# Attention logits: key low parts stored in both partition halves, and the softmax division moved behind the values' products

## The chip, the cores and the metric

The kernel runs on one core of one Trainium2 chip. The metric is device time in microseconds; the kernel before took 1897.31 us (median of 3 runs, 1897.23 to 1901.52).

## The reference, cut to what matters

The program is one layer of a hybrid decoder: a gated delta rule (mixer A), sparse attention over the 256 best keys of each query (mixer B), a merge, and an MLP. The change lies in mixer B's attention over a prompt of 1024 tokens, 8 query heads of 64 numbers, 2 key/value heads:

```python
kb = rope(rms_norm(bk.reshape(b, t, N_KV_B, HD_B), k_norm_g), pos)
...
logits = jnp.einsum('bqngd,bqknd->bqngk', qg, k_sel, preferred_element_type=jnp.float32) * (HD_B ** -0.5)
logits = jnp.where(valid[:, :, None, None, :], logits, -jnp.inf)
p = jax.nn.softmax(logits, axis=-1)
o = jnp.einsum('bqngk,bqknd->bqngd', p.astype(v.dtype), v_sel)
```

The kernel does not gather: it computes logits against all earlier keys and adds a mask that leaves out those not selected.

## The kernel before, in words

**Precision by parts.** TensorE multiplies float32r numbers here. To keep float32 accuracy each operand is kept as two parts, hi (rounded) and lo (the rest), and a product is made of several passes that add up in PSUM.

**The stages.** `mixers()` makes norms, projections, the indexer's scores and masks, and the delta rule. In it, `kv_chain` (line 495) makes keys and values by token tile of 128 rows and writes their parts to DRAM (`kvd`, 640 columns a tile). At its end `pool_chain` (line 412) loads `kvd` into the tile `kv` (lines 436 to 438). Then `rest()` (line 1601) runs the attention, the merge of the two mixers, and the MLP.

**The attention.** 16 groups (token tile t, kv head n), in the order of tiles 7, 6, 0, 1, 2, 5, 4, 3. A group of tile t has L = 128 (t + 1) keys and 4 query heads.

- `logit_chain` (line 1620): loads the queries `q3`, rotates them (`rope`, GpSimd and VectorE), transposes and splits them into `qS`. `split_heads` (line 361) puts hi on 64 partitions and lo on the other 64. For each head and each 512 keys there are two passes into the PSUM tile `pat`: line 1646 with 128 rows (query hi and lo, against key hi, which `kv` holds twice, once in each half of the partitions), and line 1648 with 64 rows (query hi against key lo; lo of kv head n lies in half n only). VectorE adds the mask and takes the maximum (line 1649). Then come, per head: the maximum of two chunks, a product of maximum and scale (line 1654), the exponential with its sum on ScalarE, a reciprocal, and a scaling of all L exponentials by it (line 1658), on ScalarE for odd heads and on VectorE for even ones.
- `value_chain` (line 1664): for each 128 keys, 4 transposes (`ptp`), a split into `ph` (ScalarE) and `pl` (VectorE), two passes into `po`. At the end ScalarE copies `po` to `oT`, and a DMA writes it to `obd`.
- `merge_chain` and the MLP read `obd` back and fill the other engines' time: `pdn<-oa` is the projection of mixer A, `pdn<-ob` that of mixer B, `pdn<-mix` the output projection.

**The order of the work.** Each engine runs its instructions in program order. That order is written by a planner, `Flow` (line 51): it holds several chains (`value_chain` first, then `logit_chain`, `pool_chain`, `merge_chain`, `norm_chain`, `mlp_chain`) and emits the first whose inputs should be there by then. It prices a step by the sizes of its outputs (lines 71 to 80) and takes 0.8 of their sum plus 0.6 us for each engine used as the step's delay (line 113). A pass over 64 rows costs the same in it as one over 128. `logit_chain` may be at most two groups ahead of `value_chain` (line 1624). All loads and stores but those of `kv` are issued by SyncE, in one queue.

Of the kernel before, what the change touches and what calls it, by code (L numbers as in the profile page):

```python
# [8 lines left out]
F32 = mybir.dt.float32  # L9
# [7 lines left out]
P = 128  # L17
# [3 lines left out]
NS = 8  # L21
NT = NP_ + NS
C0, CN, CM = (0, 384, 768), (384, 384, 264), 384                # chunks of tokens
# [6 lines left out]
FIRST, REST = [2, 0], [1]                                         # chunks of tokens in the order of the merge  # L30
# [7 lines left out]
def tok(t):  # L38
    """columns of token tile t (8: the samples)"""
    return slice(NP_, NT) if t == 8 else slice(t * P, (t + 1) * P)  # L40
# [10 lines left out]
class Flow:  # L51
    """Emits several chains of steps in one program order: a step of the first chain whose inputs should
    be there by then, by rough estimates of what each engine has been given so far."""
# [32 lines left out]
    def run(self, chains, cur):  # L86
        """chains: generators in order of priority; they yield None or an Event to wait for; each has its own pools"""
# [37 lines left out]
def program(ctx, tc, I, O, dbg=None, upto=99):  # L125
# [10 lines left out]
    xnp = ExitStack()                                             # the mixers' x and numbers  # L136
# [17 lines left out]
    def stage(name, side=None, **tags):  # L154
        """pools of one part of the program; tags: PSUM tiles by tag"""
# [8 lines left out]
    def copy(eng, out, in_, scale=None):  # L164
        """PSUM or SBUF to SBUF on ScalarE or VectorE"""
# [20 lines left out]
    def split(hi, lo, src, heng="act", leng="dve"):  # L186
        """src -> its float32r parts; lo = src - hi is exact"""
        copy(heng, hi, src)
        (V if leng == "dve" else G).tensor_tensor(lo, src, hi.bitcast(F32), OP.subtract)

    # ------------------------------------------------------------ constants
    jp = cs2.tile([P, P], I32, name="jp")                         # column - row
# [5 lines left out]
    tri = cs2.tile([P, P], F32, name="tri")                       # row <= column  # L198
# [4 lines left out]
    # ------------------------------------------------------------ weights  # L203
    def block(src, name, lo="pool", spare=False):
        """[P, kt, n] of weights -> their float32r parts, a list of [P, 2, n] by 128 rows"""
# [10 lines left out]
    def unit(src, name, lo="pool"):  # L216
        """weights in blocks of 512 numbers a partition"""
# [6 lines left out]
    def dense(ws, xin, evac, chunks=range(3)):  # L224
        """products of 128 columns of weights with all tokens, channels on partitions; a step per chunk"""
# [9 lines left out]
    # ------------------------------------------------------------ scratch in DRAM  # L235
    qd = dr.tile([8, P, 512], F32, name="qd")                     # attention queries by token tile
    qid = dr.tile([8, P, 512], F32, name="qid")                   # indexer queries by token tile
    sd = dr.tile([NS, 3, 512], F32, name="sd")                    # the samples' indexer and attention queries; k v ki
    cqd = dr.tile([12, P, NT], F32, name="cqd")                   # q, k, v of mixer A, channels on partitions
    azd = dr.tile([P, 4, NT], F32, name="azd")  # L240
    gd = dr.tile([16, P, NT], F32, name="gd")                     # the merge gates
    obd = dr.tile([2, P, 4, NP_], F32, name="obd")                # mixer B by kv head: rows of both parts of the values, head, token
# [3 lines left out]
    def oat(t):  # L246
        """mixer A's rows for a token tile"""
        c = t % 3 * P
        return oad[t // 3][:, :, c:c + (NS if t == 8 else P)]


    # ------------------------------------------------------------ kept over both mixers
    kvd = dr.tile([8, P, 640], F32, name="kvd")                   # parts of keys and values by token tile, as part 4 takes them
    off = {t: sum((u + 1) * P for u in range(2, t)) for t in range(2, 9)}
    right = {}                                                    # pools from the other end of the SBUF
    wab = cs2.tile([P, 9, 8], F32, name="wab")
    wsg = cs2.tile([P, 9, 8], F32, name="wsg")
    abt = cs2.tile([P, 9, 8], F32, name="abt")                    # logits of beta and the decay by token
    G.memset(abt[:, 8, :], 0.0)
    cs_s = cs2.tile([P, 12, NS], F32, name="cs_s")                # q, k, v of the samples in mixer A  # L260
    az_s = cs2.tile([P, 4, NS], F32, name="az_s")
    ssA = cs2.tile([P, 2, 9, 4], F32, name="ssA")                    # sums of squares of q and k heads
    G.memset(ssA[:, :, 8], 1.0)

    qsc = cst.tile([P, 9, 8], F32, name="qsc")                    # 1 / norm of the attention queries, over 8
# [10 lines left out]
    def seg(t):  # L276
        return cur["sc"][:, off[t]:off[t + 1]]                    # scores of token tiles 2..7, then their masks

    # ------------------------------------------------------------ mixer A: numbers by token and head
# [6 lines left out]
    # columns: 0 gc, 1 rk, 2 rk beta, 3 beta, 4 exp(gc); 5 -gc, 6 -rk beta exp(gc), 7 rk exp(gl - gc), 8 exp(gl)  # L286
# [3 lines left out]
    Ud = dr.tile([NCH, P * 4 * P + P], F32, name="Ud")            # padded: diagonal blocks at one stride over all chunks  # L290
    decd = dr.tile([NCH, P, 4, P], F32, name="decd")              # the decays of each chunk
# [29 lines left out]
    def xat(t):  # L321
        """x^T of token tile t: [P, parts, 128 rows, tokens]"""
# [17 lines left out]
    def gains(pool=None):  # L340
        """(q, k) gains x (plain, halves swapped)"""
# [1535 lines left out]
```

## Time and profile before

| what | value |
|---|---|
| median of 3 runs | 1897.31 us (1897.23 to 1901.52) |
| the profiled execution, its span (first to last instruction) | 1899.1 us |
| TensorE busy | 1826.1 us, 96% of the span |
| TensorE weight loads | 1719.9 us, 91% |
| VectorE / ScalarE / GpSimd busy | 58% / 45% / 32% |
| logits, first to last pass | 805.3 to 1051.8 us |

In the profile PE is TensorE's matmuls, PEld its weight loads, DVE VectorE, ACT ScalarE, POOL GpSimd, SP SyncE. Every instruction has line 82, that of the planner's recorder, so one goes by the names of tiles. Durations of PE rows are modelled and overlap: what a pass costs is read from the start of one row to the start of the next.

### The profile page before, as it was taken

To read this page: it belongs to the slowest core of one execution; us is meant where nothing else is said; L and a number is where in the kernel's file an instruction comes from. 1 tells how busy PE (TensorE), PEld (TensorE's weight loads), DVE (VectorE), ACT (ScalarE), POOL (GpSimd) and SP (SyncE) were. 2 spreads that over 40 slices of the span, in tenths; PEclk is the share of its full clock that TensorE was granted. 3 is DMA by queue.
4 is the path that set the end of the run, shared out by engine and by line. 5 is a ranking of instruction groups with operands and counts; after the bars stand their busy time and mean duration, and the time that the engine had idled before them with its cause. 6 is when DMAs were issued, how large, how long until landed. Compare 5 with 4: busy or idle time off the path is not lost. (4 is left out here: it accounts for less than half of the span.)

```text
span 1899.1 us, 32840 instructions
## 1 busy us (share of the span) xinstructions
PE 1826.1 (96%) x11894; PEld 1719.9 (91%) x11894; DVE 1109.7 (58%) x3116; ACT 852.1 (45%) x1945; POOL 609.8 (32%) x749
## 2 busy tenths in 40 slices
PE   6999989899999999999999979999999999999998
PEld 5899979898998889878777879999999999999998
DVE  7767768998897985277889677222232323232323
ACT  5356675567787522256767634222222131313131
POOL 2334336614332461301433465222222121313130
PEclk9999999999999999999899989999999999999999
DMA  5335463215354444633664453111111111111112
GB/s 179 109 100 170 150 214 111 82 55 170 107 153 119 136 135 136 204 114 113 182 173 131 119 172 95 55 46 45 45 51 50 45 45 51 41 54 46 45 34 90
DMA packets 167764, 198.24 MB, mean 104 GB/s; under 512 B 29521, under 2 KB 112769, under 8 KB 167594
## 3 DMA queue, kind: packets, MB, share of 16 engines
q1 hardware_dynamic: 163314, 183.04, 32.0%
q0 software_dynamic: 4288, 13.11, 2.4%
q8 instruction: 93, 1.52, 0.3%
q14 instruction: 69, 0.57, 0.1%
HBM read 148.99 MB, written 47.21 MB: 103 GB/s over the span
## 5 line engine op out<-in xcount | busy, mean ns | idle before, releaser
L82 PE MATMUL pdn<-u,wc 128*128 128x384 f32 (+1 forms) x2304 | 367.3, 320 | 0.0
L82 PEld LDWEIGHTS pdn<-u,wc 128*128 128x128 f32 x2304 | 362.7, 188 | 0.1
L82 PE MATMUL pdn<-hn,wc 128*128 128x384 f32 (+1 forms) x2304 | 362.1, 319 | 0.0
L82 PEld LDWEIGHTS pdn<-hn,wc 128*128 128x128 f32 x2304 | 360.5, 188 | 0.3
L82 PE MATMUL pdn<-xn,wu 128*128 128x384 f32 (+1 forms) x1440 | 256.7, 331 | 3.2 <-ACT z L82 3.2
L82 DVE TENSOR_TENSOR hT<-hT,pdn 128x384 f32<-128x384 f32 (+1 forms) x216 | 110.5, 512 | 251.1 <-PE pdn L82 248.0
L82 PEld LDWEIGHTS pdn<-xn,wu 128*128 128x128 f32 x1440 | 231.6, 194 | 11.1 <-issue 5.3
L82 DVE SCALAR_TENSOR_TENSOR r<-pdn,rs 128x384 f32<-128x384 f32 (+1 forms) x96 | 49.4, 516 | 273.6 <-PE pdn L82 273.5
L82 POOL TENSOR_TENSOR u<-r,u 128x384 fp32r<-128x384 f32 (+1 forms) x96 | 89.4, 932 | 274.3 <-ACT u L82 247.6
L82 PE MATMUL pa<-xn,wu 128*128 128x384 f32 (+1 forms) x864 | 158.0, 329 | 2.5 <-ACT a L82 2.5
L82 PEld LDWEIGHTS pa<-xn,wu 128*128 128x128 f32 x864 | 139.3, 193 | 4.5 <-ACT a L82 2.9
L82 ACT ACTIVATE r<-r 128x384 f32<-128x384 f32 (+1 forms) x96 | 47.1, 492 | 172.4 <-DVE r L82 171.7
L82 ACT ACTIVATE jka<-sc,nf 128x512 bf16<-128x512 f32 (+3 forms) x124 | 101.4, 821 | 33.5 <-DVE nf L82 19.7
L82 PE MATMUL pdn<-mix,wc 128*128 128x384 f32 (+1 forms) x576 | 96.3, 321 | 1.9 <-ACT mix L82 1.3
L82 PEld LDWEIGHTS pdn<-mix,wc 128*128 128x128 f32 x576 | 90.8, 188 | 3.6 <-ACT mix L82 1.7
L82 DVE SCALAR_TENSOR_TENSOR a<-u,cw,a 128x384 f32<-128x384 f32 (+1 forms) x108 | 76.2, 706 | 13.1 <-ACT a L82 12.4
L82 PE MATMUL pat<-kv,qS 128*128 128x512 f32 (+3 forms) x192 | 73.4, 431 | 3.2 <-DVE qS L82 3.1
L82 POOL TENSOR_TENSOR wu<-wu_4r,wu 128x512 fp32r<-128x512 f32 x32 | 42.8, 1336 | 104.3 <-ACT wu L82 96.2
L82 PE MATMUL pdn<-ob,wc 128*128 128x384 f32 (+1 forms) x288 | 57.6, 350 | 10.3 <-DVE ob L82 7.3
L82 DVE TENSOR_SCALAR_CACHE_REDUCE jk<-sc,cf 128x768 bf16<-128x768 f32 (+1 forms) x62 | 66.2, 1071 | 1.4 <-ACT jka L82 1.3
L82 PEld LDWEIGHTS pat<-kv,qS 128*128 128x128 f32 x192 | 36.4, 189 | 33.6 <-issue 25.0
L82 ACT ACTIVATE lg<-lg,st,qsc 128x1024 f32<-128x1024 f32 (+7 forms) x64 | 55.3, 864 | 22.2 <-DVE st L82 21.7
(904 smaller groups left out, 3350.8 us busy)
## 6 DMA issues: line engine op xcount, KB each, us to landing
wu_0r<-in_w_un SPq DMA_DIRECT2D x32, 256.0 KB
wu_4r<-in_w_un SPq DMA_DIRECT2D x32, 256.0 KB
gd<-g SPq DMA_DIRECT2D x32, 192.0 KB
ga<-gd SPq DMA_DIRECT2D x32, 192.0 KB
cqd<-a SPq DMA_DIRECT2D x24, 192.0 KB
xt<-in_x_prompt SPq DMA_DIRECT2D x8, 512.0 KB
obd<-oT SPq DMA_DIRECT2D x16, 256.0 KB
xt<-in_x_prompt SPq DMA_DIRECT2D x16, 256.0 KB
```

Of the source, the lines that this page charges most:

```text
L82: return f(*a, **k)
```

## The change

- Key lo parts of each kv head are stored in both halves of the partitions, like key hi. `kvd` and `kv` grow from 640 to 768 columns, with one transpose more per token tile, and the copy of the transposed keys grows from 384 to 512 columns.
- The second pass of the logits uses all 128 rows (query hi and lo against key lo), like the first.
- The queries are multiplied by their scale `qsc` on GpSimd before the rotation, so the exponential needs no scale.
- VectorE writes negated logits and takes the minimum; the second chunk starts from the first's minimum. This takes the place of two or three small VectorE instructions per head.
- The exponentials aren't divided by their sum. One reciprocal per group makes the 4 factors; `value_chain` transposes them (4 transposes of a column repeated over 128 columns), ScalarE copies them to `rb`, and VectorE multiplies `po` by `rb` where ScalarE copied before.
- Buffers: `lg` 10 to 9, `st` 3 to 4, `rb` in the place of `oT`.

The diff, without those hunks that only take out comments or rename sizes:

```diff
-                    kv = w([P, 640], "kvt", F32R)
+                    kv = w([P, 768], "kvt", F32R)
...
-                    V.tensor_tensor(kst[:, 2], ko3, kst[:, 0:2, 0].bitcast(F32), OP.subtract)
-                    split(kst[:, 3], kst[:, 4], bc(kio[:, i], 2))
+                    V.tensor_tensor(kst[:, 2:4], bc(ko3, 2, 2), kst[:, 0:2].bitcast(F32), OP.subtract)
+                    split(kst[:, 4], kst[:, 5], bc(kio[:, i], 2))
...
-                    for j in range(5):
-                        T.transpose((ptk if j < 3 else pti)[:, (j % 3) * P:(j % 3 + 1) * P],
+                    for j in range(6):
+                        T.transpose((ptk if j < 4 else pti)[:, (j % 4) * P:(j % 4 + 1) * P],
...
-                    copy("act", kv[:, :384], ptk[:, :384])
+                    copy("act", kv[:, :512], ptk)
...
+                G.tensor_tensor(q3, q3, bc(qsc[:, t, 4 * n:4 * n + 4], 64, 2), OP.mult)
                 qr = w([P, 4, 64], "qr")
                 rope(qr, q3, tab, P, 4)
-                qS = split_heads(qr, "qS", 2, n, "pa")
+                qS = split_heads(qr, "qS", 2, 0, "pa")
                 yield
-                st_ = small([P, 4, 4], "st", bufs=3)
+                st_ = small([P, 4, 4], "st", bufs=4)
...
-                        T.matmul(p3, qS[:, h], kv[:, bl, n * P:(n + 1) * P], start=True, stop=False)
-                        hi = slice(64 * n, 64 * n + 64)
-                        T.matmul(p3, qS[hi, h], kv[hi, bl, 256:384], start=False, stop=True)
-                        V.tensor_tensor_reduce(lg[:, c0:c0 + cn], pa[:, :cn], bias[:, c0:c0 + cn], 1.0, LOW,
-                                               op0=OP.add, op1=OP.max, accum_out=st_[:, c, h:h + 1])
-                    if nch == 2:
-                        V.tensor_tensor(st_[:, 0, h:h + 1], st_[:, 0, h:h + 1], st_[:, 1, h:h + 1], OP.max)
-                    scale = qsc[:, t, 4 * n + h:4 * n + h + 1]
-                    V.scalar_tensor_tensor(st_[:, 2, h:h + 1], st_[:, 0, h:h + 1], -1.0, scale, op0=OP.mult, op1=OP.mult)
-                    S.activation(lg[:, :L], lg[:, :L], AF.Exp, bias=st_[:, 2, h:h + 1], scale=scale,
-                                 accum_out=st_[:, 3, h:h + 1])
-                    V.reciprocal(st_[:, 1, h:h + 1], st_[:, 3, h:h + 1])
-                    copy("act" if h % 2 else "dve", lg[:, :L], lg[:, :L], st_[:, 1, h:h + 1])
+                        for a in range(2):
+                            T.matmul(p3, qS[:, h], kv[:, bl, (2 * a + n) * P:(2 * a + n + 1) * P], start=(a == 0), stop=(a == 1))
+                        V.tensor_tensor_reduce(lg[:, c0:c0 + cn], pa, bias[:, c0:c0 + cn], -1.0,
+                                               st_[:, c - 1, h:h + 1] if c else -LOW,
+                                               op0=OP.add, op1=OP.min, accum_out=st_[:, c, h:h + 1])
+                    S.activation(lg[:, :L], lg[:, :L], AF.Exp, bias=st_[:, nch - 1, h:h + 1], scale=-1.0,
+                                 accum_out=st_[:, 2, h:h + 1])
                     yield
+                V.reciprocal(st_[:, 3], st_[:, 2])
+                lgs.append(st_[:, 3])
...
+                pr = pst("prr", "pt")
+                for h in range(4):
+                    T.transpose(pr[:, h * P:(h + 1) * P], lgs[4][:, h:h + 1].to_broadcast([P, P]), ident)
+                rb = w([P, 512], "rb", bufs=2)
+                copy("act", rb, pr)
                 po = pst("po", "po")
...
-                oT = w([P, 512], "oT", bufs=2)
-                copy("act", oT, po)
-                dma(obd[n, :, :, tok(t)], h4(oT))
+                V.tensor_tensor(rb, po, rb, OP.mult)
+                dma(obd[n, :, :, tok(t)], h4(rb))
```

## Rows read from the trace of the kernel before

**Rows 1.** The page, part 1: busy time, share and instructions of each engine.

```profile
PE 1826.1 (96%) x11894; PEld 1719.9 (91%) x11894; DVE 1109.7 (58%) x3116; ACT 852.1 (45%) x1945; POOL 609.8 (32%) x749
```

**Rows 2.** Windows of the attention: length, busy of PE, PEld, DVE, ACT, POOL, clock, DMA.

```profile
840.00:880.00 40.00, 40.00 (x212) 30.71 (x210) 31.91 (x97) 28.70 (x49) 3.46 (x4) 1.00 0.33 102
...
930.00:980.00 50.00, 49.37 (x294) 38.28 (x293) 46.43 (x134) 36.76 (x78) 18.82 (x18) 1.00 0.63 176
...
sum 270.00, PE 262.63 PEld 209.93 DVE 217.67 ACT 182.20 POOL 72.68; mean PE 43.77 PEld 34.99 DVE 36.28 ACT 30.37 POOL 12.11
```

**Rows 3.** Tile pat: matmuls, ns min/median/max, first and last start, forms (rows*columns).

```profile
L82 PE MATMUL pat<-kv,qS x192: 221/440/687, 805.5 to 1051.8; 128*128 128x512 f32 x48, 64*128 64x512 f32 x48, 128*128 128x384 f32 x16, 64*128 64x384 f32 x16
```

**Rows 4.** Timeline, tile 7's first head: start, length, engine, operation, count, idle before.

```profile
805.49 2.53 PE L82 MATMUL pat<-kv,qS 128*128 128x512 f32 x6
...
805.80 0.18 PEld L82 LDWEIGHTS pat<-kv,qS 64*128 64x128 f32 x1 [0.30 <-issue]
...
807.94 2.04 PEld L82 LDWEIGHTS pdn<-oa,wc 128*128 128x128 f32 x12 [0.24 <-DVE st L82]
807.94 2.35 PE L82 MATMUL pdn<-oa,wc 128*128 128x384 f32 x12
```

**Rows 5.** Timeline of PE alone: chunks of 128 keys, transposes, chunks of 384 keys.

```profile
892.82 1.58 PE L82 MATMUL pat<-kv,qS 128*128 128x128 f32 x6
894.34 1.73 PE L82 MATMUL pdn<-oa,wc 128*128 128x264 f32 x12
...
940.94 1.27 PE L82 MATMUL ptp<-ident,lg 128*128 128x128 f32 x10
941.97 2.27 PE L82 MATMUL pat<-kv,qS 128*128 128x384 f32 x6
944.16 1.72 PE L82 MATMUL pdn<-ob,wc 128*128 128x264 f32 x12
```

**Rows 6.** Timeline of PE alone, the indexer's scores (psc), next to other products.

```profile
404.00 1.09 PE L82 MATMUL psc<-kiS,qiS 128*128 128x512 f32 x4
404.93 2.19 PE L82 MATMUL pqb<-wbq,xn 128*128 128x256 f32 x17
```

**Rows 7.** Tile lg: the transposes of the exponentials, ns min/median/max.

```profile
L82 PE MATMUL ptp<-ident,lg x288: 270/272/331, 816.7 to 1069.5; 128*128 128x128 f32 x144
```

**Rows 8.** Tiles st and lg: what goes; and groups by line: a product from PSUM.

```profile
L82 DVE SCALAR_TENSOR_TENSOR st<-st,qsc x64: 133/157/981, 808.9 to 1055.1; 128x1 f32<-128x1 f32 x64
L82 DVE RECIPROCAL st<-st x64: 146/157/165, 811.6 to 1058.7; 128x1 f32<-128x1 f32 x64
...
L82 DVE TENSOR_SCALAR lg<-lg,st x32: 275/554/1626, 813.3 to 1058.3; 128x1024 f32<-128x1024 f32 x4, 128x896 f32<-128x896 f32 x4, 128x128 f32<-128x128 f32 x4, 128x256 f32<-128x256 f32 x4
L82 ACT ACTIVATE lg<-lg,st x32: 393/762/1153, 817.4 to 1059.4; 128x1024 f32<-128x1024 f32 x4, 128x896 f32<-128x896 f32 x4, 128x128 f32<-128x128 f32 x4, 128x256 f32<-128x256 f32 x4
...
L82 DVE TENSOR_TENSOR pl<-ptp,ph 128x512 fp32r<-128x512 f32 x72 | 48.6, 683 | 4.6 <-ACT ph L82 4.3
```

**Rows 9.** Tile qr: GpSimd's product and its wait; SyncE's wait for it (us, times, longest).

```profile
L82 POOL TENSOR_TENSOR qr<-q,tab x15: 718/734/1034, 802.9 to 1028.9; 128x256 f32<-128x256 f32 x15
...
  PE ptq L82: 81.8, 13
...
SPq L1628 <- POOL qr L82: 13.9, 9, 4.8
```

**Rows 10.** Tile kv: its load, issue and landing; window in which the keys are made.

```profile
L438 POOL DMA_DIRECT2D kv<-kvd x8: 540/540/646, 760.0 to 763.8; - x8
...
DMA to landing us min/median/max: 6.6/7.9/9.3
...
50.00:100.00 50.00, 45.77 (x334) 42.85 (x332) 34.58 (x123) 18.20 (x48) 19.32 (x25) 0.97 0.33 107
```

**Rows 11.** Two windows in which TensorE waits; columns as in rows 2.

```profile
903.00:924.00 21.00, 17.09 (x63) 12.01 (x61) 13.92 (x51) 11.49 (x34) 7.68 (x9) 0.67 0.56 166
...
1089.00:1113.00 24.00, 12.12 (x60) 9.91 (x60) 16.73 (x30) 8.77 (x23) 15.55 (x13) 0.86 0.50 146
```

More of the change, by code (lines that the diff above doesn't have):

```diff
@@ L29 @@
 WB = (5, 2)
+LG = 9
 FIRST, REST = [2, 0], [1]
@@ L249, in oat @@
         return oad[t // 3][:, :, c:c + (NS if t == 8 else P)]
-    kvd = dr.tile([8, P, 640], F32, name="kvd")
+    kvd = dr.tile([8, P, 768], F32, name="kvd")
     off = {t: sum((u + 1) * P for u in range(2, t)) for t in range(2, 9)}
@@ L435, in pool_chain @@
             pools["G"].close()
-            cur["kv"] = kv = other("kv", [P, 8, 640], F32R)
+            cur["kv"] = kv = other("kv", [P, 8, 768], F32R)
             for t in range(8):
@@ L549, in kv_chain @@
                     ko3 = ko4[:, i]
-                    kv = w([P, 640], "kvt", F32R)
+                    kv = w([P, 768], "kvt", F32R)
                     v3 = kvo[:, i, 128:256].rearrange("p (h c) -> p h c", h=2)
-                    v4 = kv[:, 384:].rearrange("p (n a c) -> p n a c", n=2, a=2)
+                    v4 = kv[:, 512:].rearrange("p (n a c) -> p n a c", n=2, a=2)
                     split(v4[:, :, 0], v4[:, :, 1], v3, "act", "pool")
-                    kst = w([P, 5, 2, 64], "kst", F32R, 2)
+                    kst = w([P, 6, 2, 64], "kst", F32R, 2)
                     copy("act", kst[:, 0:2], bc(ko3, 2, 2))
-                    V.tensor_tensor(kst[:, 2], ko3, kst[:, 0:2, 0].bitcast(F32), OP.subtract)
-                    split(kst[:, 3], kst[:, 4], bc(kio[:, i], 2))
+                    V.tensor_tensor(kst[:, 2:4], bc(ko3, 2, 2), kst[:, 0:2].bitcast(F32), OP.subtract)
+                    split(kst[:, 4], kst[:, 5], bc(kio[:, i], 2))
                     ptk, pti = pst("ptk", "pa"), pst("pti", "pa")
-                    for j in range(5):
-                        T.transpose((ptk if j < 3 else pti)[:, (j % 3) * P:(j % 3 + 1) * P],
+                    for j in range(6):
+                        T.transpose((ptk if j < 4 else pti)[:, (j % 4) * P:(j % 4 + 1) * P],
                                     kst[:, j].rearrange("p a c -> p (a c)").bitcast(F32), ident)
-                    copy("act", kv[:, :384], ptk[:, :384])
+                    copy("act", kv[:, :512], ptk)
                     copy("dve", kiS[:, :, tok(t)], pti[:, :256].rearrange("p (a c) -> p a c", a=2))
@@ L1630, in logit_chain @@
                     tab = q_rows(t, gt)
+                G.tensor_tensor(q3, q3, bc(qsc[:, t, 4 * n:4 * n + 4], 64, 2), OP.mult)
                 qr = w([P, 4, 64], "qr")
                 rope(qr, q3, tab, P, 4)
-                qS = split_heads(qr, "qS", 2, n, "pa")
+                qS = split_heads(qr, "qS", 2, 0, "pa")
                 yield
-                st_ = small([P, 4, 4], "st", bufs=3)
+                st_ = small([P, 4, 4], "st", bufs=4)
                 lgs = []
+                nch = (L + 511) // 512
@@ L1637, in logit_chain @@
                 for h in range(4):
-                    lg = w([P, NP_], "lg", bufs=10)
+                    lg = w([P, NP_], "lg", bufs=LG)
                     lgs.append(lg)
-                    nch = (L + 511) // 512
                     for c in range(nch):
                         c0, cn = c * 512, min(512, L - c * 512)
-                        pa = pst("pat", "pa")
-                        p3 = pa[:, :cn].rearrange("p (b k) -> p b k", k=P)
+                        pa = pst("pat", "pa")[:, :cn]
+                        p3 = pa.rearrange("p (b k) -> p b k", k=P)
@@ L1674, in value_chain @@
                     split(ph, pl, pt)
-                    vb = kv[:, b, 384 + n * P:384 + (n + 1) * P]
+                    vb = kv[:, b, 512 + n * P:512 + (n + 1) * P]
                     T.matmul(po, vb, ph, start=(b == 0), stop=False)
```

## Prediction

> **What bounds the kernel now.** I read the page first: TensorE is busy 96% of the span and no other engine over 58% [rows 1], so a change pays where it shortens TensorE's own queue. Then the windows of the attention, 805 to 1075 us: TensorE 262.6 of 270 us, VectorE 217.7, ScalarE 182.2 [rows 2]. In its fullest part (930 to 980) VectorE has 46.4 of 50 us beside TensorE's 49.4, so VectorE is a near second and must be followed too. Last the tile of the logits and the timeline around it, since a busy TensorE need not be a fast one. There are 192 logits passes, half over 128 rows and half over 64, in turn [rows 3]; by the chunks of the 16 groups they are 96 passes of 512 keys and 32 each of 384, 256 and 128.
>
> The timeline shows what they cost. Six passes of 512 keys start at 805.49 and the next work at 807.94: 0.408 us a pass. Between passes of different row counts the weight load starts only 0.30 us after the load before it ended. The 12 projections behind them, all over 128 rows, take 2.35 us, 0.196 us for 384 columns, and their 12 loads follow each other without idle time [rows 4]. The same surcharge stands on short chunks: 1.52 us for six passes of 128 keys (892.82 to 894.34), 0.253 each, and 2.19 us for six of 384, 0.365 each [rows 5]. It is about as long for 128 keys as for 512, so it is no slow stream but something paid once a pass: a load that doesn't hide behind the pass before. The twin that the change would make exists already: the indexer's scores multiply the same kind of hi/lo queries, both passes over 128 rows, 512 columns: four passes from 404.00 to 404.93, 0.232 us each [rows 6].
>
> **The change part by part.**
>
> *Logits passes.* All rows alike, so I take the twin's price. 512 keys: 0.408 - 0.232 = 0.176 us, x 96 = 16.9. 384 keys: 0.365 less the projections' 0.196 [rows 4, 5] = 0.169, x 32 = 5.4. 128 keys: no float32r pass that short is among my rows; the transposes' pace of 0.103 (ten in 1.03 us) [rows 5] is nearest, as they too load 128 columns and stream 128: 0.150, x 32 = 4.8. 256 keys lie between: 0.17 x 32 = 5.4. Sum: 32.5 us off TensorE. Bounds: nothing, if the loads stay serial, and 34, if short passes go at half the transposes' pace.
>
> The Trainium skill, in "TensorE: Matmul & The Clock Gate", Part 3, speaks against it: a weight load overlaps matmuls in flight only when the row groups differ, and here the change makes them all the same. By that rule the 32.5 us would be zero. The trace disagrees with it: 12 loads over the same 128 rows run on without idle time [rows 4], so the measured row decides and the rule stands below as a rival.
>
> *Transposes of the factors.* 4 per group, 64 in all, on TensorE: 64 x 0.103 = 6.6 us. Their operand is one column read 128 times, which no row shows; bounds are zero (done while TensorE waits) and the recorded length, 64 x 0.272 = 17.4 us [rows 7]. I take 0.103, since for the transposes of `lg` starts lie that far apart though each lasts 0.272.
>
> *Keys.* 8 transposes more, 0.8 us by the same pace, at 50 to 147 us, where TensorE has idle time (45.8 of 50 us) [rows 10]; 0 to 2 us with the longer copy and store, I take 0.8. The load of `kv` grows by a fifth: it is issued at 760 and lands 7.9 us later [rows 10], over 30 us before the first pass at 805.5 [rows 3], so a fifth more is hidden by that gap. Nothing.
>
> *VectorE and ScalarE.* VectorE loses 64 products and 64 reciprocals of 0.157 us and 32 scalings of 0.554, together 37.8 us, and the maxima on top; it gains 16 reciprocals and 16 products from PSUM, priced as `pl`, 0.683: 13.4 us [rows 8]. Net -24 us or more of 217.7. ScalarE loses 32 scalings of 0.762, 24.4 us [rows 8]; the copy of `rb` takes the place of that of `oT`. Neither sets the end, so I count these at nothing; what they do is keep VectorE below TensorE: about 193 against 236 us over the stage (262.6 - 32.5 + 6.6). That the minimum's second chunk starts from a register just written could add a short wait in 32 places on VectorE, which has this room.
>
> *GpSimd.* 16 products of q3, 0.73 us as `qr` [rows 9], 0 to 12 us. I take nothing: GpSimd sits idle 81.8 us before its `qr` products waiting for `ptq`, that is for a free buffer [rows 9], and the new product needs only the loaded queries, so it runs in that wait. Queued behind it are weights' low parts; SyncE, which already waits 13.9 us for these products before loading queries [rows 9], may wait up to 0.7 us a group more, and loads of weights and gates stand behind that in its queue. They are issued blocks ahead.
>
> *Added waits.* The reciprocal waits for the last head's exponential; behind it on VectorE stand `pl` splits and mask additions, 16 times instead of 64. The product with `po` moves to VectorE's queue: behind it waits SyncE's store to `obd`, and the next group's first pass into the only `po` buffer, which has 8 transposes and a split ahead of it as cover. `lg` with 9 buffers costs nothing: a group starts only after the values' steps of the group two before are in TensorE's queue.
>
> *Sum:* -32.5 + 6.6 + 0.8 = -25.1 us. The profiled span of 1899.1 us becomes 1874.0; the median is 1.8 us lower, and 1897.3 - 25.1 = **1872.2 us**. What is late next: TensorE still, 236 us of work in a stage of about 245.
>
> **The rivals.**
>
> *Half is given back in waits.* The stage has a second chain, mask addition, exponential, transposes, split. If TensorE, now quicker, outruns it, time turns into waits on VectorE. For it: 46.4 of 50 us in the fullest window [rows 2]; an in-order queue whose planner does not know the true prices. Against: VectorE sheds as much as TensorE there. Price: half of 25.1, so 1885. It decides once TensorE's idle time in the stage grows beyond about 20 us from 7.4.
>
> *Holes close as well.* TensorE is short of work at 903 to 924 (17.1 of 21 us, granted clock 0.67, so at 1.2 instead of 2.4 GHz for two thirds of it) and at 1089 to 1113 (12.1 of 24) [rows 11], when a value round trip through DRAM ends and no filler is left. The planner now prices a head cheaper (no scaling, fewer small steps), so it emits less filler between heads, and more is left for the holes. Against: at large tiles the planner's pace is that of `value_chain`, hardly changed. Price: half of the 3.9 + 11.9 idle us and some of the slow clock, 12 us: 1860.
>
> *Loads stay serial: slower.* If the weight load waits for the pass before for another reason (the same row groups, as the skill's page has it, or the strided keys), 128 rows twice cost 0.408 again. Then only additions are left: 1897.3 + 6.6 + 0.8 = 1904.7. It decides when a pass saves less than 7.4 / 192 = 0.039 us, that is above 0.37 us for 512 keys. Against: rows 6, the same passes at 0.232. This is also the case in which the change does not do what it says.
>
> **How the numbers follow.** Forecast 0.62 (within 5 us of 1872); half given back 0.19; holes close 0.13; serial loads 0.04; 0.02 for no change by some other cover. Range 1856 to 1886: it takes in the first three and the bounds of the transposes and the keys nearly whole (+10.8 and +1.2 us), and leaves out the serial case and sums of mishaps. What this kernel's measurement can tell from no change is about 0.3%, 5.7 us. Faster by more: the first three cases less a tail of the second, 0.91. Within: 0.05. Slower: 0.04.
>
> **What would show it.** Right: `pat` passes of 512 keys start 0.23 us apart, loads of `pat` without the 0.24 to 0.30 us before them, all in 128-row form; 64 `prr` transposes some 0.1 us apart; TensorE's work between the first pass and the last `po` down by 25 us with its idle time about as before; VectorE at most 200 us there; and the MLP unchanged. Wrong: passes still 0.4 us apart; or passes fast, but TensorE idle before `po` and `ptp`, released by VectorE, or before `pdn`, released by weights (SyncE behind its store to `obd`). Holes at the places of rows 11 that are shorter than now would put the time below 1867.

## The result and the profile after

The changed kernel takes 1876.1 us (median of 4 runs, 1872.7 to 1878.7) against 1898.9 us for the kernel before (median of 4 runs; the 1897.31 us ahead of the prediction was over the first three of them): -22.8 us, ratio 0.9876 with a 95% interval of 0.9861 to 0.9892. Measured again later it was 0.9869 (0.9852 to 0.9887). Forecast were 1872.2 us, a ratio of 0.987, within 1856 to 1886.

The page after, its first line, part 1 and the clock line of part 2, against rows 1:

```profile
span 1870.9 us, 32909 instructions
...
PE 1790.5 (96%) x11966; PEld 1715.5 (92%) x11966; DVE 1091.9 (58%) x2956; ACT 830.3 (44%) x1917; POOL 613.8 (33%) x765
...
PEclk9999999999999999999899999999999999999999
```

TensorE has 35.6 us less to do, though it has 72 instructions more. Its share of the span is the same 96%: it is still what bounds the kernel.

Windows of both kernels, from the first logits pass to the last `po`, and from there to the first product of the MLP (length, busy of PE, PEld, DVE, ACT, POOL, clock, DMA). First before, then after:

```profile
805.50:1071.70 266.20, 258.83 (x1424) 206.12 (x1424) 217.50 (x643) 179.18 (x373) 70.86 (x67) 0.97 0.48 140
1071.70:1162.50 90.80, 77.01 (x415) 72.75 (x414) 67.45 (x100) 44.66 (x100) 57.20 (x46) 0.94 0.50 152
```

```profile
806.30:1043.70 237.40, 224.66 (x1453) 205.41 (x1453) 186.50 (x482) 149.64 (x341) 75.44 (x80) 0.96 0.51 152
1043.70:1134.30 90.60, 80.50 (x438) 75.57 (x437) 73.12 (x104) 45.92 (x101) 59.72 (x47) 0.98 0.52 159
```

The attention is 28.8 us shorter, all of the 28.2 us between the two profiled executions; the rest of the merge keeps its length, and the MLP takes 736.6 and 736.7 us. The forecast for the attention alone was 25.9. VectorE fell to 186.5 us, the forecast being 193. TensorE's busy time in the attention fell by 34.2 us, and its idle time rose from 7.4 to 12.7.

These two executions lie further apart than the medians do: the one before is the longest of its four, the one after the shortest of its four. So 28.8 us is what this pair shows, and 22.8 us is what the change is worth.

The timeline of TensorE after: a head of tile 7's second group, the first factors, and the weight loads of other heads. It answers rows 4 and rows 7:

```profile
816.53 1.08 PE L83 MATMUL pat<-kv,qS 128*128 128x512 f32 x4
817.45 2.28 PE L83 MATMUL pdn<-oa,wc 128*128 128x384 f32 x12
819.56 0.60 PE L83 MATMUL prr<-ident,st 128*128 128x128 f32 x4
820.00 1.04 PE L83 MATMUL ptp<-ident,lg 128*128 128x128 f32 x8
...
810.30 1.28 PEld L83 LDWEIGHTS pat<-kv,qS 128*128 128x128 f32 x6
```

Four passes of 512 keys take 0.92 us, 0.23 each: the price of the indexer's twin [rows 6]. Six loads follow each other in 1.28 us; the 0.24 to 0.30 us ahead of each load are gone. Over all 192 loads of `pat` the idle time before them fell from 33.6 to 6.1 us. The transposes of the factors start 0.11 us apart.

The first hole of rows 11 is still there, some 15 us earlier. A stretch of 25 us around it, before and then after, and the end of the merge after:

```profile
900.00:925.00 25.00, 21.09 (x92) 15.42 (x92) 17.85 (x62) 14.76 (x42) 9.92 (x11) 0.73 0.56 169
...
885.00:910.00 25.00, 17.76 (x102) 15.14 (x101) 15.10 (x46) 11.26 (x34) 11.09 (x13) 0.73 0.64 190
...
1061.00:1085.00 24.00, 16.10 (x84) 14.08 (x83) 19.43 (x28) 9.21 (x23) 17.74 (x15) 0.93 0.59 169
```

The granted clock is 0.73 in both, but TensorE is idle for 7.2 us of the 25 where it was 3.9. At the end of the merge it is the other way: 7.9 us of 24 idle and a clock of 0.93, where it was 11.9 us and 0.86 [rows 11]. The rest of the merge is as long as before all the same, since more of TensorE's work falls into it (80.5 against 77.0 us).

Ahead of the first hole the attention lost 14.0 us (97.6 to 83.6, from the first pass to the last product of mixer A), behind it 15 us. And who let TensorE wait within the attention (us, times, longest):

```profile
PE pdn L83 <- ACT ob L83: 3.1, 1, 3.1
PE ptp L83 <- ACT rb L83: 3.0, 1, 3.0
PE pat L83 <- DVE qS L83: 2.1, 2, 1.5
PE po L83 <- DVE pl L83: 1.7, 3, 0.8
```

The second is new: once, for 3.0 us, the transposes of the exponentials waited for the copy of the factors out of PSUM, a wait that the forecast did not name.

### The profile page after: what moved, and what is told of

It is laid out like the page before. It is cut to its first block, busy times and chain, and to the rows that moved or that the text cites. A ratio compares the mean times of both kernels' runs of the same rounds, so it can differ in the third digit from the quotient of the medians.

```text
span 1870.9 us, 32909 instructions
## 1 busy us (share of the span) xinstructions
PE 1790.5 (96%) x11966; PEld 1715.5 (92%) x11966; DVE 1091.9 (58%) x2956; ACT 830.3 (44%) x1917; POOL 613.8 (33%) x765
## 4 chain that ended last, share of the span: by engine, by line
PE 45%; DMA 2%; DVE 2%; POOL 1%; issue 1%; ACT 0%; SPq 0%; ACTq 0%; POOLq 0%; DVEq 0%
PE pdn L83 42%; PE po L83 1%; PE ptp L83 1%; PE pat L83 1%; PE pty L83 0%; POOL wc L83 0%; DMA wc28r<-in_w_o 0%; DMA wc64r<-in_w_o 0%; DVE rs L83 0%; DVE wc L83 0%; DMA ld<-obd 0%; PE ptx L83 0%; DVE ga L83 0%; POOL ssq L83 0%; DMA wc58r<-in_w_b 0%
## 5 line engine op out<-in xcount | busy, mean ns | idle before, releaser
L83 PE MATMUL pdn<-xn,wu 128*128 128x384 f32 (+1 forms) x1440 | 250.8, 325 | 0.9 <-ACT z L83 0.9
L83 PEld LDWEIGHTS pdn<-xn,wu 128*128 128x128 f32 x1440 | 224.7, 189 | 9.1 <-issue 4.6
L83 PE MATMUL pdn<-mix,wc 128*128 128x384 f32 (+1 forms) x576 | 100.6, 328 | 4.5 <-DVE wc L83 2.2
L83 PE MATMUL pqb<-wbq,xn 128*128 128x256 f32 (+1 forms) x432 | 59.1, 286 | 0.0
L83 ACT ACTIVATE lg<-lg,st 128x1024 f32<-128x1024 f32 (+7 forms) x64 | 49.3, 772 | 21.1 <-DVE st L83 19.7
L83 PEld LDWEIGHTS pdn<-ob,wc 128*128 128x128 f32 x288 | 46.9, 196 | 11.9 <-ACT ob L83 5.4
```

What stands on the lines that cost most here:

```text
L83: return f(*a, **k)
```

## The experiments

All ratios are to the kernel before, measured beside them on the same chip. The first four kernels of the table ran on one chip, the next four on a second, the last four on a third. The kernel before had medians of 1898.7, 1900.5 and 1899.7 us there, and differences in us below are to the median of its own chip.

| kernel | us | ratio (95%) |
|---|---|---|
| the changed kernel again | 1875.9 | 0.9869 (0.9852 to 0.9887) |
| rows part alone | 1885.7 | 0.9927 (0.9913 to 0.9941) |
| changed, second pass over 64 rows | 1903.4 | 1.0026 (1.0014 to 1.0037) |
| changed, exponentials scaled as before | 1880.1 | 0.9896 (0.9880 to 0.9911) |
| keys part alone | 1908.8 | 1.0047 (1.0028 to 1.0066) |
| changed, first stage in another order | 1881.4 | 0.9903 (0.9882 to 0.9925) |
| 64-row passes grouped | 1899.3 | 0.9998 (0.9984 to 1.0012) |
| changed, no division | 1876.6 | 0.9875 (0.9854 to 0.9896) |
| changed, both passes over 64 rows | 1895.6 | 0.9984 (0.9968 to 1.0000) |
| before with 9 `lg` buffers | 1901.7 | 1.0015 (0.9999 to 1.0031) |
| changed, keys doubled by DMA | 1879.4 | 0.9903 (0.9880 to 0.9926) |
| the same, factors later | 1880.4 | 0.9904 (0.9883 to 0.9926) |

### Which part brought the gain

The reference point on the same chip:

> The changed kernel again, on the same chip as the three beside it, so that they can be compared with it. Expected as measured before: 1876 us, ratio to the kernel before 0.988 (0.986 to 0.989).

Measured 1875.9 us, as expected. In its profile the first product of mixer A's projection starts at 799.1 us, not at 790.4, and from there to the MLP it took 342.3 us, not 343.9. So two executions of the same program differ by 8.7 us ahead of the attention; the attention itself, from the first pass to the last `po`, took 234.9 us, not 237.4. Below, a difference of 9 us ahead of the attention or of 3 us within it, between one profile and another, can be no more than this.

**Rows alone.**

> The kernel before with the rows part alone: key lo parts in both halves of the partitions, all logits passes over 128 rows, lg with 9 buffers; softmax as before. Theory A (the passes' serial weight loads set the time): TensorE loses 32.5 us and gains 0.8 for the keys, so 1899 - 31.7 = 1867 us, faster than the full change by its 64 transposes of factors, 6.6 us, unless VectorE, unrelieved at 218 us of a stage of some 240, takes part of it back (up to 1876). Theory B (the relief of VectorE and ScalarE brought the gain, the passes were hidden by waits for VectorE anyway): 1890 us or more.

```diff
-                qS = split_heads(qr, "qS", 2, n, "pa")
+                qS = split_heads(qr, "qS", 2, 0, "pa")
...
-                        T.matmul(p3, qS[:, h], kv[:, bl, n * P:(n + 1) * P], start=True, stop=False)
-                        hi = slice(64 * n, 64 * n + 64)
-                        T.matmul(p3, qS[hi, h], kv[hi, bl, 256:384], start=False, stop=True)
+                        for a in range(2):
+                            T.matmul(p3, qS[:, h], kv[:, bl, (2 * a + n) * P:(2 * a + n + 1) * P], start=(a == 0), stop=(a == 1))
```

Measured 1885.7 us: -13.0, under half of the 31.7 that theory A gave without VectorE, and 10 us over the worst that it allowed. Most of those 10 us are not VectorE's: theory A put the keys at 0.8 us, and by themselves, with 9 `lg` buffers, they cost 8.3 (keys alone, below). Its windows and waits, as above:

```profile
809.10:1057.20 248.10, 227.25 (x1424) 204.38 (x1424) 209.96 (x644) 176.16 (x374) 68.46 (x67) 0.97 0.50 150
...
PE pat L82 <- DVE qS L82: 6.3, 6, 1.8
PE po L82 <- ACT ph L82: 4.8, 4, 2.1
PE ptx L82 <- DMA xt<-in_x_prompt: 3.9, 3, 2.4
```

TensorE's work shrank as far as in the changed kernel (227.3 against 224.7 us), but the stage did not: 20.9 us of it TensorE is idle, for the most part behind VectorE's splits of the queries and ScalarE's splits of the exponentials. That these are late because of the softmax work in the same queues is argued, not shown: the kernel without any division, below, waits 7.6 us for the queries' splits too.

**Softmax alone.**

> The changed kernel with one edit undone: the second logits pass again over 64 rows (query hi, key lo), all else as changed, so the small lo by lo products are left out as before. Theory A: TensorE has the 32.5 us back and keeps the transposes of the factors, 1876 + 32.5 = 1908 us, slower than the kernel before by 5 to 10. Theory B: 1885 or less, since VectorE and ScalarE stay relieved.

```diff
-                        for a in range(2):
-                            T.matmul(p3, qS[:, h], kv[:, bl, (2 * a + n) * P:(2 * a + n + 1) * P], start=(a == 0), stop=(a == 1))
+                        T.matmul(p3, qS[:, h], kv[:, bl, n * P:(n + 1) * P], start=True, stop=False)
+                        T.matmul(p3, qS[:64, h], kv[:64, bl, (2 + n) * P:(3 + n) * P], start=False, stop=True)
```

Measured 1903.4 us, 4.7 over the kernel before; theory A said 5 to 10, theory B is out. The attention is back at 262.2 us although VectorE is as relieved as in the changed kernel:

```profile
810.90:1073.10 262.20, 256.05 (x1452) 206.80 (x1451) 192.11 (x481) 151.46 (x340) 76.60 (x80) 0.97 0.47 138
```

The larger keys and the 9 `lg` buffers are in both of these kernels and in the changed one, so the kernel to set them against is keys alone (below), and not the kernel before; otherwise what the keys cost is counted in each. The four side by side (us; the last three columns from the profiles, from the first logits pass to the last `po`):

| kernel | against the kernel before | attention | TensorE busy | TensorE idle |
|---|---|---|---|---|
| keys alone | +8.3 | 271.4 | 258.0 | 13.4 |
| with the rows | -13.0 | 248.1 | 227.3 | 20.9 |
| with the softmax | +4.7 | 262.2 | 256.1 | 6.2 |
| with both (changed) | -22.8 | 237.4 | 224.7 | 12.7 |

So the rows bring 21.3 us by themselves, the softmax edits 3.6, and both together 31.1. Some 6 us belong to the pair, with an uncertainty of about 6 us when the four intervals are added as squares; in the attention of the profiles only 1.5 us of 34.0 belong to it, and 4.0 of 36.5 with the second profile of the changed kernel. All of these lean on one kernel, keys alone, measured on another chip. The columns say why the parts nearly add up. The rows take 31 us of work off TensorE, with the softmax edits or without, and add about 7 us of waits. The softmax edits take off 7 to 8 us of waits, with the rows or without.

**Where the division stands.**

> The changed kernel with the division put back where it was: a reciprocal and a scaling of the exponentials per head (VectorE for even heads, ScalarE for odd), no transposes of factors, no product with po. Theory A: TensorE loses 6.6 us (64 transposes of 0.103), VectorE gains 48 reciprocals and 32 scalings less 16 products, about +14 us net, and has room: 1869 us. Rival (VectorE is the near second and binds once TensorE is quick): 1880 us or more, with TensorE idle before ptp and po, released by VectorE or ScalarE.

```diff
+                    V.reciprocal(st_[:, 3, h:h + 1], st_[:, 2, h:h + 1])
+                    copy("act" if h % 2 else "dve", lg[:, :L], lg[:, :L], st_[:, 3, h:h + 1])
                     yield
...
-                V.tensor_tensor(rb, po, rb, OP.mult)
+                rb = w([P, 512], "rb", bufs=2)
+                copy("act", rb, po)
```

Measured 1880.1 us, 4.2 over the changed kernel, with intervals that overlap: the rival's side. Its window and longest waits:

```profile
811.10:1052.90 241.80, 226.03 (x1413) 203.77 (x1412) 199.19 (x549) 170.35 (x374) 79.44 (x82) 0.96 0.52 152
...
PE pat L83 <- DVE qS L83: 4.8, 5, 2.1
PE ptx L83 <- DMA xt<-in_x_prompt: 3.4, 2, 2.8
```

VectorE has 12.7 us more than in the changed kernel and ScalarE 20.7, but TensorE waits for the queries' splits and hardly, as the rival had it, before `ptp` (1.2 us) and `po`. The 64 transposes are the cheaper place for the division. From rows alone to this kernel, which has all the softmax edits but the division, it is between 5 and 6 us, and from here to the changed kernel 4.2. The next kernel asks what the division still costs:

> The changed kernel without any division by the sum of the exponentials (left out: the reciprocals, the 64 transposes of the factors, the copy to rb, the product with po; ScalarE copies po as before). It measures what the division costs where it now stands. By the prediction 64 x 0.103 = 6.6 us of TensorE, so 1869 us; if the waits that it adds (ptp behind the copy rb held 3.0 us in the changed kernel) come on top, 1866; if it hides in TensorE's idle time, 1873 or more.

```diff
-                pr = pst("prr", "pt")
-                for h in range(4):
-                    T.transpose(pr[:, h * P:(h + 1) * P], lgs[4][:, h:h + 1].to_broadcast([P, P]), ident)
-                rb = w([P, 512], "rb", bufs=2)
-                copy("act", rb, pr)
...
-                V.tensor_tensor(rb, po, rb, OP.mult)
+                rb = w([P, 512], "rb", bufs=2)
+                copy("act", rb, po)
```

Measured 1876.6 us: nothing gained that can be told, the third of the branches. The windows of the profiled execution, the same two stretches as in the profile after:

```profile
808.40:1038.00 229.60, 214.14 (x1365) 194.83 (x1364) 181.81 (x448) 148.10 (x335) 75.37 (x79) 0.96 0.52 154
1038.00:1136.40 98.40, 86.32 (x462) 80.81 (x461) 74.95 (x107) 50.33 (x108) 62.27 (x50) 0.97 0.50 157
```

The attention ends 7.8 us earlier, and the rest of the merge is 7.8 us longer. Over both windows TensorE works 4.7 us less than in the changed kernel and the sum stays at 328.0: what is taken off comes back as waits, 7.6 us of them of logits passes for the queries (2.1 in the changed kernel).

### What a pass over 64 rows costs

**Grouping.**

> The changed kernel with the second pass over 64 rows, as in e2_64rows, but with the passes of a head's two chunks grouped: both over 128 rows, then both over 64 rows. Of tiles 4 to 7, 128 passes, half of the changes of row count go: 64. Theory C (paid at each change of row count): 64 x 0.176 = 11 us off e2_64rows, 1892, and 64-row passes of 512 keys behind each other start 0.23 us apart. Theory D (a 64-row pass is slow whatever stands before it): as e2_64rows, 1903, and those starts 0.4 us apart.

```diff
+                    for c, c0, cn, pa, p3, bl in cks:
+                        T.matmul(p3, qS[:, h], kv[:, bl, n * P:(n + 1) * P], start=True, stop=False)
+                    for c, c0, cn, pa, p3, bl in cks:
+                        T.matmul(p3, qS[:64, h], kv[:64, bl, (2 + n) * P:(3 + n) * P], start=False, stop=True)
```

Measured 1899.3 us, between the two theories, because the edit was largely undone: the build places instructions by simulated times (line 1865), and in the trace most passes stand in turn again. Counted over TensorE's rows of the trace, the changes of row count next to `pat` fell from 192 to 168, not to 128. The 24 that went are 4.2 us at 0.176 each; against the kernel before this kernel is at -1.2 us and softmax alone, with 192, at +4.7. The few 64-row passes of 512 keys behind each other (12) start 0.34 us apart, which is neither theory's 0.23 nor 0.4.

**Both passes over 64 rows.**

> The changed kernel with both logits passes over the same 64 rows (query hi against key hi, query hi against key lo; query lo against key hi is left out): 64 rows everywhere in pat, no change of row count inside a head. If the surcharge is paid at changes of row count: passes of 512 keys start 0.23 us apart and the time is that of the changed kernel, 1876. If it belongs to 64-row passes: 0.34 us apart, as the few neighbouring 64-row passes of e3_grouped, 192 x 0.11 = 21 us more, 1897.

```diff
-                            T.matmul(p3, qS[:, h], kv[:, bl, (2 * a + n) * P:(2 * a + n + 1) * P], start=(a == 0), stop=(a == 1))
+                            T.matmul(p3, qS[:64, h], kv[:64, bl, (2 * a + n) * P:(2 * a + n + 1) * P], start=(a == 0), stop=(a == 1))
```

Measured 1895.6 us, near the 1897 of the second branch, and the median distance of neighbouring passes of 512 keys is 0.337 us, as that branch had it. But the timeline (TensorE alone) shows that it doesn't belong to each pass:

```profile
816.22 1.65 PE L83 MATMUL pat<-kv,qS 64*128 64x512 f32 x6
817.80 1.73 PE L83 MATMUL pdn<-oa,wc 128*128 128x264 f32 x12
...
826.49 0.73 PE L83 MATMUL pat<-kv,qS 64*128 64x512 f32 x2
827.16 0.79 PE L83 MATMUL pdn<-oa,wc 128*128 128x384 f32 x3
...
829.12 0.50 PE L83 MATMUL pat<-kv,qS 64*128 64x512 f32 x1
829.56 0.51 PE L83 MATMUL po<-ph,kv 128*128 128x512 f32 x1
829.99 0.50 PE L83 MATMUL pat<-kv,qS 64*128 64x512 f32 x1
830.42 0.50 PE L83 MATMUL po<-pl,kv 128*128 128x512 f32 x1
```

Over 0.232 us a pass, a run of six costs 0.19 us more, one of two 0.20, a single one 0.20: the surcharge is paid at the ends of a run, not for each pass. Pass by pass, the run of six starts 0.337, 0.236, 0.229, 0.232, 0.226 and 0.323 us apart, and the 128-row projection just ahead of it takes 0.269 us where 0.173 is usual for 384 columns. So a change costs about 0.2 us, half of it at the pass before it and half at the pass behind. A `po` pass over 128 rows between two 64-row passes has a change on each side and takes 0.43 us where it else takes 0.23. Most runs of this kernel are two passes long, with the price of a change in each, and that is the median of 0.337. It belongs to the change of row count. The expectation overlooked that a head's passes stand between 128-row work of other chains: 136 changes were left. The windows of the attention in the grouped kernel, then in this one:

```profile
813.00:1070.90 257.90, 250.89 (x1454) 204.82 (x1453) 192.01 (x481) 151.30 (x341) 76.11 (x79) 0.98 0.47 139
...
809.40:1067.10 257.70, 248.67 (x1457) 203.33 (x1457) 190.60 (x481) 152.27 (x341) 77.43 (x81) 0.97 0.48 141
```

Over the changed kernel's 237.4 us this one has 20.3 us, 0.15 us a change; with 192 changes (softmax alone) it is 24.8 us, 0.13 a change; with 168 (grouped) 20.5, 0.12. Three kernels give 0.12 to 0.15 us a change on the path, as near to each other as single profiles allow, and the changed kernel has no change in `pat`.

### What the keys cost

**Keys alone.**

> The kernel before with the keys part alone: low parts in both halves (768 columns, one more transpose per tile), the second pass still over 64 rows, softmax as before. By the prediction: +0.8 us, 1899.5, no change that can be told. Rival: in the four profiles with the larger keys the indexer's scores end 10 to 14 us later than in the kernel before and the merge's first product starts 2 to 8 us later than at 791.1, since every engine's order in the first 440 us is another one; then +4 us, 1903, with all of it ahead of the attention.

```diff
-                    V.tensor_tensor(kst[:, 2], ko3, kst[:, 0:2, 0].bitcast(F32), OP.subtract)
+                    V.tensor_tensor(kst[:, 2:4], bc(ko3, 2, 2), kst[:, 0:2].bitcast(F32), OP.subtract)
...
-                        T.matmul(p3, qS[hi, h], kv[hi, bl, 256:384], start=False, stop=True)
+                        T.matmul(p3, qS[hi, h], kv[hi, bl, (2 + n) * P:(3 + n) * P], start=False, stop=True)
```

Measured 1908.8 us, +8.3, where the prediction had 0.8 and the rival 4. The kernel differs from the one before in one more thing, which the text above does not say: it has 9 `lg` buffers in the place of 10. Its attention:

```profile
807.50:1078.90 271.40, 258.04 (x1425) 204.94 (x1424) 217.62 (x644) 179.25 (x373) 70.81 (x67) 0.98 0.46 138
```

That is 5.2 us more than in the profile before, with the same passes; 2.1 us lie ahead of it and 0.5 in the rest of the merge. So the rival's place, all of it ahead of the attention, is wrong for the greater part. Three kernels looked for the cause.

> The kernel before with 9 lg buffers in place of 10, nothing else. By the prediction no change: 1899 to 1900. Rival: part of the 8 us that e7_keys lost lies in the attention (271 us from the first pass to the last po, against 266) and comes from the buffer taken away: 1904.

```diff
-                    lg = w([P, NP_], "lg", bufs=10)
+                    lg = w([P, NP_], "lg", bufs=9)
```

Measured 1901.7 us, +2.0, ratio 1.0015 with an interval that holds 1 and reaches 5.9 us. Its profiled execution was the longest of 12, 1911.5 us, and there the attention is as long as in keys alone:

```profile
809.90:1081.40 271.50, 259.59 (x1425) 206.97 (x1425) 214.58 (x643) 179.09 (x373) 68.81 (x67) 0.97 0.47 137
```

So the buffer may be the 5 us of the attention or, by the median, only a part of them; one profile of an unusual execution does not settle it.

> The changed kernel with the additional work on the keys (one transpose, 128 columns of a subtraction and of a copy per tile) left out of the planner's prices; the work is the same, only the order of the instructions in the first stage is another. If the first stage's loss is the keys' own work: 1876 as before. If it is the order that the additions happen to bring: another value, between 1870 and 1880, all of the difference ahead of the attention.

```diff
-                        T.transpose((ptk if j < 4 else pti)[:, (j % 4) * P:(j % 4 + 1) * P],
+                        (nc.tensor if j == 3 else T).transpose((ptk if j < 4 else pti)[:, (j % 4) * P:(j % 4 + 1) * P],
...
-                    copy("act", kv[:, :512], ptk)
+                    nc.scalar.activation(kv[:, :512], ptk, AF.Copy)
+                    flow.used["act"] = flow.used.get("act", 0.0) + 0.2 + 384 / 1200.0
```

Measured 1881.4 us, -19.1 against the kernel before where the changed kernel has -22.8. All its 6 runs are longer than all 8 of the changed kernel's, but on another chip, and the intervals just overlap (0.9882 to 0.9925 and 0.9852 to 0.9887). So another order of the same work may be worth some 4 us; it is not settled. In the profile the attention is as long as in the changed kernel, 237.6 us.

> The changed kernel, but key low parts are made and stored once, as in the kernel before (640 columns), and reach both halves of the partitions in the loads ahead of the attention: 16 + 4 DMAs from GpSimd's queue in the place of 8. Every engine's order up to the attention is then that of the kernel before. If the keys' part cost 4 to 5 us ahead of the attention: 1871. If not, 1876. If the 20 loads come too late for the first pass (33 us of room before), 1880.

```diff
-            for t in range(8):
-                nc.gpsimd.dma_start(kv[:, t], kvd[t])
+            src = kvd.rearrange("t p c -> p t c")
+            for t in range(8):
+                nc.gpsimd.dma_start(kv[:, t, :256], kvd[t, :, :256])
+                nc.gpsimd.dma_start(kv[:, t, 512:], kvd[t, :, 384:])
+            for n in range(2):
+                for x in range(2):
+                    nc.gpsimd.dma_start(kv[64 * x:64 * x + 64, :, (2 + n) * P:(3 + n) * P], src[64 * n:64 * n + 64, :, 256:384])
```

Measured 1879.4 us: with the keys' work and, but for the loads, the order ahead of the attention those of the kernel before, nothing came back. The last loads were issued at 779.4 us and the first pass started at 815.3, so they were not late. The attention is as long as in the changed kernel, 237.5 us; the rest of the merge took 95.6 us in place of 90.6, in a profiled execution of 1886.8 us, 7 above the median.

All profiles together say the same. Four have, on TensorE, VectorE and ScalarE, the order of the kernel before up to the start of the merge (before, 9 `lg` buffers, this kernel and the next): mixer A's first product starts at 791.1, 794.2, 799.4 and 791.3 us, 794.0 on average. Nine have the larger keys and share one order up to there (all others but the one in another order): 790.4 to 799.1 us, 794.4 on average. The scores do end 10 to 15 us later in those nine, but no loss is left at the start of the merge. The rival of keys alone, 2 to 8 us later, had set four profiles against a single one and left out the profile after, which starts at 790.4.

> e11_dma_keys with the transposes of the factors half-way through a group's values instead of ahead of them, so that the first ptp no longer waits for the copy rb (3.0 us in the changed kernel) nor for the reciprocal. Expected 0 to 3 us below e11_dma_keys; if TensorE's wait only moves, the same.

```diff
+                    if b == t // 2:
+                        pr = pst("prr", "pt")
+                        for h in range(4):
+                            T.transpose(pr[:, h * P:(h + 1) * P], lgs[4][:, h:h + 1].to_broadcast([P, P]), ident)
+                        rb = w([P, 512], "rb", bufs=2)
+                        copy("act", rb, pr)
                     yield
```

Measured 1880.4 us, the same. It could not show what it was for: the wait of `ptp` for `rb` is not in its trace, but it is not in that of the kernel it was set against either. It has others, among them 2.3 us of `po` for ScalarE's split. No version beat the changed kernel.

## Why the prediction came out right, point by point

**The sum** came out, -25.1 against -22.8 us, but its terms did not, and that is luck: the misses are 7 to 11 us and cancel. The measured terms come from the four kernels of the table above:

| term | forecast | measured |
|---|---|---|
| logits passes over 128 rows | -32.5 | -21.3 |
| softmax edits, the transposes of the factors among them | +6.6 | -3.6 |
| larger keys, and 9 `lg` buffers | +0.8 | +8.3 |
| the pair of rows and softmax | 0 | -6.2 |
| sum | -25.1 | -22.8 |

Of the signs that the prediction named, one did not come: TensorE's idle time in the attention is not about as before, but 12.7 us against 7.4.

**The logits passes**, -32.5 us of TensorE: right in size and cause as work, but not as time. Passes of 512 keys start 0.23 us apart (forecast 0.232). In the trace after, the median starts are 0.176 us apart for 384 keys (the forecast's 0.196 took the length of the last of 12 projections with it), 0.120 for 256 and 0.112 for 128; with these and 0.2325 for 512 all 192 passes come to 35.4 us without waits, against 36.3 by the prediction's prices. TensorE's busy time fell by 30.8 us from keys alone to rows alone. Of these 7.5 us came back as idle time in the attention, where the sum has all of them as time saved. The rule that the prediction quotes from the Trainium skill ("TensorE: Matmul & The Clock Gate", Part 3), that a weight load overlaps matmuls in flight only when the row groups differ, does not hold for these passes. By it nothing would be gained, and here six loads over the same 128 rows follow each other in 1.28 us behind running passes. What is paid lies at changes of row count, as the experiments with 64 rows show; the prediction left open whether it is the change or the pass.

**The transposes of the factors**, +6.6: 0.11 us each, as forecast, but not on the path. Without the division nothing is gained (1876.6 us). The step that failed is that TensorE's work was taken for time: with the passes quick, the stage has waits into which a few microseconds of TensorE's work fit.

**VectorE and ScalarE**, counted at nothing: wrong as a term. The softmax edits bring 3.6 us without the rows and, with their transposes paid, 9.8 beside them (1885.7 to 1875.9); in the profiles they take 7 to 8 us off TensorE's idle time. The prediction's first rival, half given back in waits, with 1885 us and TensorE idle some 20 us, looks like rows alone, 1885.7 us and 20.9 us idle. But that agreement is chance in part: 13.4 of the idle us stand in keys alone already, and what the rows gave back is a quarter of TensorE's saving, not half.

**The keys**, +0.8, and **the `lg` buffer**, nothing: together 8.3 us in the kernel before. What the prediction said of the keys' own work, that it costs hardly anything ahead of the attention, is borne out as far as the profiles go: no loss is left at the start of the merge, and taking the work out of the first stage brought nothing back. Of the loss 5.2 us stand in the attention, where the buffer or the order of the instructions, which the build works out anew for each kernel, could be the cause. Neither is shown; by medians the buffer explains 2.0 us, and 5.9 at the end of its interval.

**The rest.** The bigger load of `kv` was hidden, as forecast. The product on GpSimd showed no wait of its own: TensorE waited 2.1 us for the queries where it was 3.1 before; it was not tried by itself, nor was the minimum in the place of the maximum. The holes, which the forecast left as they were, changed by +3.3 and -4.0 us of idle time without a change in the length of the rest of the merge. The MLP is unchanged.

## What to carry to other kernels

When passes over different numbers of rows alternate on TensorE, look at the idle time ahead of the weight loads: fill the short pass up to the full rows, even with products that aren't needed, or keep equal rows together (argued from the runs of passes above, since the one try was largely undone); then look in the trace whether the build left them together. A gain on the bounding engine is worth what the other engines let through, here three quarters of it, so cost their relief as a term of its own. When parts of a change are tried one by one, set each against a kernel that has everything else that comes with it: against the kernel before, the rows seemed to bring 13.0 us and the softmax edits to cost 4.7, where against keys alone they bring 21.3 and 3.6. And look at several executions before you place a few microseconds: two of the same program were 8.7 us apart ahead of the attention.

## What the runs showed of the hardware that was not expected

A change of row count between two matmuls costs both neighbours, about 0.1 us each. In the kernel with 64 rows everywhere in the logits, a 128-row `po` pass between two 64-row passes took 0.43 us in place of 0.23, and a single 64-row pass 0.43 as well, while six 64-row passes in a row took 0.26 us each, and those inside the run 0.226 to 0.236. Half the rows never made a pass quicker: among the logits passes of 512 columns 0.226 us was the shortest distance of two 64-row starts in that kernel, and 0.225 of two 128-row starts in the changed one.
